# A mixture-of-experts stage with 32 slots per token tile: one gather for six pairs, one scatter product for both halves

## The chip, the cores and the metric

The kernel runs on one core of a Trainium2 chip. The metric is the time of one execution on the device, in microseconds (us); below, times of instructions are in us or ns as each row says. Engines are named as in the profile: PE is TensorE, DVE is VectorE, ACT is ScalarE, POOL is GpSimd, SP is the engine that issues nearly all DMAs here.

## What is computed

A two-layer decoder trunk over 256 tokens of width 1024, in float32. In each layer a token mixer (three head groups, one input and one output projection) is followed by a layer norm, and then by a mixture of 16 experts, each with a gate, an up and a down matrix, which this change is about:

```python
def moe_ffn(h, router_w, router_bias, w_gate, w_up, w_down):
    t = h.reshape(B * L, D)                      # 256 x 1024
    scores = jax.nn.sigmoid(t @ router_w)
    ...                                          # best group of 4 experts, then top 2 in it
    combine = ...                                # 256 x 16, two weights per token
    out = jnp.zeros_like(t)
    for e in range(N_EXPERTS):                   # 16; D_FF = 512
        act = jax.nn.silu(t @ w_gate[e]) * (t @ w_up[e])
        out = out + combine[:, e:e + 1] * (act @ w_down[e])
```

Each of the 16 experts has 6 MB of weights per layer, so some 200 MB of expert weights pass through the core in one execution.

## The kernel before

The tokens stand in two tiles of 128 (`NT = 2`, index `t`). Experts are taken in eight pairs `p` (experts 2p and 2p + 1). A token's place among the tokens of its expert is its slot (`pos`); `CAP` slots per expert are computed (64 for all 256 tokens), so that a pair has 128 slots, and tokens over the cap go through `overflow()` (line 1397), a branch that is taken only if some expert has more than `CAP` tokens.

For a pair, PE's queue has, in this order:

- **gather**: one-hot matrices `G` (token by slot, built on DVE by `slots`) bring the tokens' rows into slot order, transposed, as `xT`. Pairs 0 and 1 have one gather each in plain float32 (`gather`, line 1337). Pairs 2 and 3, 4 and 5, 6 and 7 are gathered two at a time (`gather_two`, line 1316): h is split once into a high and a low half (`halve`), each product is made for both halves, 32 products of 256 columns per gather. ACT and DVE evict the result from PSUM with the norm's gain and offset.
- **gate and up** (tile `gu`): for each of the eight k, two products, one per expert, run side by side in the two column halves of the array, 512 columns each.
- `sT`, two transposes that turn the one-hot matrix to slot by token (`by_slot`); DVE makes it 0/1 and sums the slots' weights into `ws`.
- `aT`, four transposes of silu(gate) * up (`turn`), evicted by ACT as `actT`.
- **down** (tile `y`): 16 products of 512 columns. ACT evicts y * ws rounded (`yt`, high), DVE the rest (`yt`, low) (`split`, line 533).
- **scatter** (tile `sc`, line 1383): for each token tile and each half of the 1024 columns, the transposed one-hot times high and low, two products each (`place`), then DVE adds the result to `z`. The scatter of pair p is put into pair p + 1 (`late`), between its up and its down stage; that of pair 6 stands in the gate stage of pair 7, at `SC_AT`.

Weights come in tiles of 512 KB, 24 per pair: 8 for gate, 8 for up, 8 for down. Most go through a feed of 33 buffers (`fp`, `NFEED`, tile `wf`). `specs` (line 285) fixes their order: all gate tiles of a pair, then up, then down, then the next pair; `more()` issues the next load each time PE is through with a tile, from SP, in that order, and a load waits until its buffer has been read. Some tiles are listed in `EXTRA` instead: `more_extra` loads them during the end of the token mixer into other buffers (tile `wx`), where they wait until they are used. A `wx` tile that PE consumes frees no feed buffer. PE needs two gate tiles for each two steps k (one per expert):

```python
for k in range(KT):
    if k % 2 == 0:
        us = [feed.pop((l, nm, p, k + e)) for e in range(2)]
    for e in range(2):
        mm(b_[64 * e:64 * e + 64], xs[p](k, e), part(us[e], k % 2), ...)
        if k % 2 and type(us[e]) is not list:
            more()
```

PSUM has eight banks, taken in turn by all of these (`bank`). All PE, DVE and ACT instructions are recorded through one helper, so that every row of the profile names its line (L231); the tiles tell them apart. A plain float32 product appears as two MATMUL records, a rounded one or a transpose as one.

Of the kernel before, what the change touches and what calls it, by code (L numbers as in the profile page):

```python
# [17 lines left out]
P = 128  # L18
D = 1024
# [7 lines left out]
CAP = 64  # L27
# [14 lines left out]
EXTRA = ((1, 'd', 1, '22', -4), (1, 'g', 0, '22', -4), (2, 'g', 3, '22', -2), (1, 'g', 2, '4', -1), (1, 'g', 6, '4', -1), (1, 'd', 6, '22', 0), (0, 'u', 3, '22', 2), (0, 'd', 4, '22', 5), (0, 'g', 5, '4', 5), (0, 'u', 0, '22', 6), (2, 'd', 6, '22', 7), (2, 'd', 0, '22', 7), (1, 'd', 4, '22', 7), (2, 'u', 4, '22', 9), (1, 'u', 3, '4', 9), (2, 'd', 1, '4', 9), (2, 'g', 1, '4', 9))  # L42
# [16 lines left out]
TWO = (2, 4, 6)  # L59
AT = {(1, 'g'): 'h', (6, 'u'): 'r'}  # L60
# [175 lines left out]
def trunk_kernel(ctx, tc, x, positions, w_in, gate_up, gate_bias, norm_gain, w_out, ln_mix_g, ln_mix_b,  # L236
# [165 lines left out]
    iota = cp.tile([P, CAP], F32, name="iota")  # L402
    nc.gpsimd.iota(iota, pattern=[[1, CAP]], base=0, channel_multiplier=0, allow_small_or_imprecise_dtypes=True)
    pref = cp.tile([P, E], F32, name="pref")
    nc.gpsimd.iota(pref, pattern=[[-1, E]], base=E, channel_multiplier=0, allow_small_or_imprecise_dtypes=True)
# [7 lines left out]
    rc = cp.tile([P, NT, 16], F32, name="rc")  # L413
    rs = cp.tile([P, NT, 2, 8], F32, name="rs")

    def trig_tables():
# [44 lines left out]
        for i in range(2):  # L461
            dve.tensor_copy(rc[:, :, 8 * i:8 * i + 8], trig4[:, 1])
# [53 lines left out]
    def rope(y, off, nh, t):  # L516
        v = y[:, off:off + nh * 64].rearrange("p (h d) -> p h d", d=64)
        sw = bass.AP(tensor=y.tensor, offset=y.offset + off + 8, ap=[y.ap[0], [64, nh], [-8, 2], [1, 8]])
        ab = t1("rope", (P, 2, 128))
        ra, rb_ = (ab[:, i, 0:nh * 16].rearrange("p (h j) -> p h j", h=nh) for i in range(2))  # L520
        dve.tensor_mul(ra, v[:, :, 0:16], rc[:, t, None, :].to_broadcast([P, nh, 16]))
# [159 lines left out]
    def finish(z, sb, sts, g, b):  # L681

        mv = [sm("mv", 5) for _ in range(NT)]
# [35 lines left out]
    for l in range(DEPTH):  # L719
# [513 lines left out]
        def residual(t, n):  # L1233

            c = slice(512 * n, 512 * n + 512)
            r = whole(t, c)
            dve.scalar_tensor_tensor(r, r, ALPHA, vecs[0][:, c], op0=OP.mult, op1=OP.mult)
            dve.scalar_tensor_tensor(r, vecs[1][:, c], ALPHA, r, op0=OP.mult, op1=OP.add)
            dve.tensor_add(z[t][:, c], z[t][:, c], r)
# [6 lines left out]
        def choose(t):  # L1246
# [24 lines left out]
            else:  # L1271
                mm(pc[:, E:2 * E], strict, hot[:, E:2 * E], start=True, stop=False)
                mm(pc[:, E:2 * E], ones_b, hot[:, 0:E], start=False, stop=True)
# [6 lines left out]
        xs, Gs = {}, {}  # L1280
# [4 lines left out]

        def slots(p, tiles=range(NT), G=None):

            two = p in TWO
            n = 4 if two else 2
            if G is None:  # L1290
                G = t2("G", (P, NT, n, CAP), F32R) if two else t1("G", (P, NT, n, CAP))
            for t in tiles:
                ps_ = pos[:, t * E + 2 * p:t * E + 2 * p + n][:, :, None].to_broadcast([P, n, CAP])
                dve.tensor_tensor(G[:, t], iota[:, None, :].to_broadcast([P, n, CAP]), ps_, op=OP.is_equal)
            for q in range(n // 2):
                Gs[p + q] = (G.bitcast(F32) if two else G)[:, :, 2 * q:2 * q + 2]
            return G

        his, los = [], []

        def halve(t, n):

            c = slice(512 * n, 512 * n + 512)
            if n == 0:
                his.append(t4("hi", (P, D), F32R))
                los.append(t4("lo", (P, D), F32R))
            split(h[t][:, c], his[t][:, c], los[t][:, c])
            if n == 1:
                h[t] = None

        def whole(t, c):
            r = t2("whole")
            dve.tensor_add(r, his[t].bitcast(F32)[:, c], los[t].bitcast(F32)[:, c])
            return r

        def gather_two(p, G):

            xT = [t4("xT", (P, 4, 2 * P)) for _ in range(2)]
            for kk in range(4):
                b_ = bank("xT")  # L1320
                b3 = b_.rearrange("p (a n) -> p a n", a=2)
                for k in (2 * kk, 2 * kk + 1):
                    for i, part in enumerate((his, los)):
                        for t in range(NT):
                            mm(b3[:, k % 2], block(part[t], k), G[:, t].rearrange("p a b -> p (a b)"),
                               start=i + t == 0, stop=i + t == 2)
                for k in (2 * kk, 2 * kk + 1):
                    g_, c_ = affine(k)
                    if kk % 2 == 0:
                        act.activation(xT[k // 4][:, k % 4], b3[:, k % 2], AF.Identity, scale=g_, bias=c_)  # L1330
                    else:
                        dve.tensor_scalar(xT[k // 4][:, k % 4], b3[:, k % 2], g_, c_, op0=OP.mult, op1=OP.add)
                od.free(b_)
            for q in range(2):
                xs[p + q] = lambda k, e, o=q * P: xT[k // 4][:, k % 4, o + 64 * e:o + 64 * e + 64]

        def gather(p, G, between=None):

            xT = t4("xT", (P, KT, P))
            bs = [bank("xT") for _ in range(2)]  # L1340
            parts = [(kk, range(NT)) for kk in range(2)] if p else [(kk, (t,)) for t in range(NT) for kk in range(2)]
            for i, (kk, tiles) in enumerate(parts):
                b3 = bs[kk].rearrange("p (a n) -> p a n", a=4)
                for k in range(4):
                    for t in tiles:
                        mm(b3[:, k], block(h[t], 4 * kk + k),
                           G[:, t].rearrange("p a b -> p (a b)"), start=t == 0 and (p > 0 or k == 0), stop=t == NT - 1)
                if NT - 1 in tiles:
                    for k in range(4):
                        g_, c_ = affine(4 * kk + k)  # L1350
                        if kk == 0:
                            act.activation(xT[:, 4 * kk + k], b3[:, k], AF.Identity, scale=g_, bias=c_)
                        else:
                            dve.tensor_scalar(xT[:, 4 * kk + k], b3[:, k], g_, c_, op0=OP.mult, op1=OP.add)
                    od.free(bs[kk])
                if between and i == 0:
                    between()
            xs[p] = lambda k, e: xT[:, k, 64 * e:64 * e + 64]

        def weights(p):  # L1360
            Gw = t1("Gw", (P, NT, 2, CAP))
            for t in range(NT):
                cs_ = comb[:, t * E + 2 * p:t * E + 2 * p + 2][:, :, None].to_broadcast([P, 2, CAP])
                dve.tensor_mul(Gw[:, t], Gs[p][:, t], cs_)
            return Gw

        def by_slot(Gw):

            b_ = bank("sT")
            for t in range(NT):  # L1370
                tr(b_[:, t * P:(t + 1) * P], Gw[:, t].rearrange("p a b -> p (a b)"))
            sT = t1("sT", (P, L), F32R)
            ws = sm("ws", 1)
            dve.tensor_scalar(sT, b_[:, 0:L], 0.0, None, op0=OP.is_gt)
            dve.tensor_reduce(ws, b_[:, 0:L], AX.X, OP.add)
            od.free(b_)
            return sT, ws

# [4 lines left out]
        def scatter(p, yt, sT, tiles=range(NT)):  # L1383
            if p == 0:
                z.extend(t4("z", (P, D)) for _ in range(NT))
            for t in tiles:
                for n in range(2):
                    b_ = bank("sc")
                    place(b_, t, n, yt, sT)
                    zs = z[t][:, 512 * n:512 * n + 512]  # L1390
                    if p == 0:
                        act.activation(zs, b_, AF.Copy)
                    else:
                        dve.tensor_add(zs, zs, b_)
                    od.free(b_)

        def overflow():
            banks = [bank("ov") for _ in range(6)]
            turns = itertools.cycle(banks)
            with tc.If(rmax > CAP):  # L1400
                hTo = [t2("hTo", (P, 2, L)) for _ in range(4)]
                for t in range(NT):
                    for kk in range(2):
                        ht = whole(t, slice(512 * kk, 512 * kk + 512)).rearrange("p (q i j) -> p q j i", j=2, i=P)
# [8 lines left out]
                for e in range(E):  # L1413
# [22 lines left out]
                    for n in range(2):  # L1436
# [6 lines left out]
                        for t in range(NT):  # L1443
                            zs = z[t][:, 512 * n:512 * n + 512]
# [14 lines left out]
        G = slots(0, (0,))  # L1459

        def second():
            for _ in steps[1]:
                pass
            slots(0, (1,), G)

        gather(0, G, second)
        mm(pc[:, 2 * E:3 * E], ones_b, hot[:, 0:E], start=True, stop=False)
        mm(pc[:, 2 * E:3 * E], ones_b, hot[:, E:2 * E], start=False, stop=True)
# [8 lines left out]
        dve.tensor_reduce(cnt, pc[:, 2 * E:3 * E], AX.X, OP.max)  # L1477
# [3 lines left out]
        late = None  # L1481
# [6 lines left out]
        def begin(t, n):  # L1488
            sb[t, n] = bank("sc")
            mm(sb[t, n], ident, z[t][:, 512 * n:512 * n + 512], start=True, stop=False)  # L1490

        for p in range(E // 2):
            gu = []
            if p == E // 2 - 1:
                Gw = weights(p)
            for nm in ("g", "u"):
                b_ = bank("gu")
# [151 lines left out]
```

## Time and profile before

| | us |
|---|---|
| median of 3 runs (746.40 to 746.79) | 746.45 |
| the profiled execution | 745.53 |
| its span, first to last instruction | 743.8 |
| PE busy in the span | 715.8 |
| DVE busy | 373.4 |
| ACT busy | 255.0 |

Busy time is counted per engine over the span. A matmul's record covers its way through the array, so that records of products that follow each other overlap; where the cost of one more product is wanted, it is the distance between starts that counts. The DMA share of a stretch is the mean busy share of the core's 16 DMA engines.

### The profile page before, as it was taken

The page shows a single profiled execution, that of the slowest core. Times are in us where ns is not written, and L with a number is a line of the kernel's source. Part 1 is how long each engine was busy: PE and PEld are TensorE (multiplying, and loading weights), DVE is VectorE, ACT ScalarE, POOL GpSimd, SP SyncE. Part 2 cuts the span into 40 slices and gives each one's busy share as a digit, 9 for nine tenths or more (in the row PEclk, how much of TensorE's full clock was granted, in tenths as well). Part 3 has the DMA queues.
Part 4 walks back from the last instruction along what each step waited for, and adds up shares of the span by engine and source line. Part 5 has one row for each costly group of instructions (what it writes and reads, how often), then busy time and mean ns, then how long its engine had stood idle before and what let it go on. Part 6 is the DMA issues. An engine that isn't in the chain of part 4 may idle for free. (4 is left out here: it accounts for less than half of the span.)

```text
span 743.8 us, 11218 instructions
## 1 busy us (share of the span) xinstructions
PE 715.8 (96%) x3941; PEld 419.2 (56%) x3941; DVE 373.4 (50%) x986; ACT 255.0 (34%) x527; POOL 43.4 (6%) x67
## 2 busy tenths in 40 slices
PE   7999999999999999999899999999999999999993
PEld 6897977754533533433388888777435344353331
DVE  5887866632312322561488688666231223336405
ACT  5667655422211201210186665563222111111101
POOL 2000001100000002200130000001000000020002
PEclk9999999999999999999999999999999999999997
DMA  8899836889999999999999654569898999999941
GB/s 299 281 392 408 322 135 214 325 312 371 364 343 410 408 410 408 408 409 400 332 387 351 221 176 143 195 207 360 316 380 334 367 408 409 409 408 408 406 177 56
DMA packets 81519, 243.04 MB, mean 327 GB/s; under 512 B 9956, under 2 KB 14120, under 8 KB 81448
## 3 DMA queue, kind: packets, MB, share of 16 engines
q1 hardware_dynamic: 80776, 241.86, 86.2%
q8 instruction: 36, 0.59, 0.3%
q10 hardware_dynamic: 416, 0.26, 0.1%
q14 instruction: 35, 0.29, 0.1%
q0 software_dynamic: 256, 0.03, 0.0%
HBM read 241.08 MB, written 1.05 MB: 326 GB/s over the span
## 5 line engine op out<-in xcount | busy, mean ns | idle before, releaser
L231 PE MATMUL gu<-wf,xT 128*64 128x512 f32 x944 | 224.3, 593 | 3.0 <-PEq L1400 3.0
L231 PEld LDWEIGHTS gu<-wf,xT 128*64 128x64 f32 x944 | 72.8, 137 | 136.8 <-issue 126.9
L231 DVE TENSOR_TENSOR wlo<-wf,whi 128x512 fp32r<-128x512 f32 (+2 forms) x174 | 97.3, 598 | 39.6 <-ACT whi L231 36.9
L231 PE MATMUL y<-wf,actT 128*64 128x512 f32 x456 | 110.7, 596 | 1.4 <-ACT actT L231 1.4
L231 ACT ACTIVATE whi<-wf 128x512 fp32r<-128x512 f32 (+2 forms) x176 | 86.8, 552 | 14.5 <-PE po L231 9.5
L231 DVE TENSOR_TENSOR act<-act,gu 128x512 f32<-128x512 f32 x16 | 11.0, 687 | 141.9 <-PE gu L231 86.5
L231 PE MATMUL pj<-whi,hhi 128*128 128x512 f32 (+2 forms) x224 | 81.7, 365 | 0.0
L231 PE MATMUL pj<-wlo,hhi 128*128 128x512 f32 (+2 forms) x224 | 78.2, 349 | 1.6 <-DVE wlo L231 1.5
L231 PE MATMUL pj<-whi,hlo 128*128 128x512 f32 (+2 forms) x224 | 77.7, 347 | 0.0
L231 DVE SCALAR_TENSOR_TENSOR yt<-y,ws,yt 128x512 fp32r<-128x512 f32 x32 | 23.8, 750 | 106.6 <-ACT yt L231 105.4
L231 PEld LDWEIGHTS y<-wf,actT 128*64 128x64 f32 x456 | 33.8, 137 | 58.5 <-issue 51.8
L231 ACT ACTIVATE yt<-y,ws 128x512 fp32r<-128x512 f32 x32 | 21.8, 688 | 100.6 <-PE y L231 100.1
L231 PEld LDWEIGHTS pj<-whi,hhi 128*128 128x128 f32 x224 | 42.1, 188 | 8.3 <-issue 2.9
L231 PEld LDWEIGHTS pj<-wlo,hhi 128*128 128x128 f32 x224 | 42.2, 188 | 7.1 <-DVE wlo L231 3.4
L231 PEld LDWEIGHTS pj<-whi,hlo 128*128 128x128 f32 x224 | 42.1, 188 | 5.2
L231 ACT ACTIVATE xT<-xT,cols 128x256 f32<-128x256 f32 (+1 forms) x40 | 18.2, 518 | 72.0 <-PE xT L231 72.0
L231 PE MATMUL sc<-yt,sT 128*128 128x512 f32 x128 | 36.7, 414 | 1.8 <-ACT yt L231 1.7
L231 ACT ACTIVATE act<-gu 128x512 f32<-128x512 f32 x16 | 9.6, 597 | 79.5 <-PE gu L231 67.0
L231 PE MATMUL gu<-wx,xT 128*64 128x512 f32 x80 | 36.6, 592 | 0.0
L231 ACT ACTIVATE actT<-aT 128x512 f32<-128x512 f32 x16 | 9.6, 598 | 70.0 <-PE aT L231 70.0
L231 DVE TENSOR_TENSOR z<-z,sc 128x512 f32<-128x512 f32 x48 | 29.7, 679 | 7.7 <-PE sc L231 7.7
L231 PEld LDWEIGHTS sc<-yt,sT 128*128 128x128 f32 x128 | 21.9, 189 | 12.5 <-issue 4.9
(269 smaller groups left out, 966.1 us busy)
## 6 DMA issues: line engine op xcount, KB each, us to landing
wf<-in_w_expert_up_dram SPq DMA_DIRECT2D x120, 512.0 KB, 9.6
wf<-in_w_expert_gate_dram SPq DMA_DIRECT2D x116, 512.0 KB, 7.6
wf<-in_w_expert_down_dram SPq DMA_DIRECT2D x114, 512.0 KB, 10.1
wf<-in_w_in_dram SPq DMA_DIRECT2D x32, 512.0 KB, 9.8
wf<-in_w_out_dram SPq DMA_DIRECT2D x16, 512.0 KB, 10.3
wx<-in_w_expert_down_dram SPq DMA_DIRECT2D x24, 256.0 KB, 6.0
wf<-in_w_in_dram SPq DMA_DIRECT2D x16, 292.0 KB, 5.9
wf<-in_w_in_dram SPq DMA_DIRECT2D x16, 264.0 KB, 4.9
```

Source lines behind the costliest of these rows:

```text
L231: return fn(*a, **kw)
```

## The change

Each expert has 32 slots for each token tile (`CAP = 32`, a pair still has 4 x 32 = 128 slots). So a gather's product for token tile t fills only the slots of t, and nothing is added up over tiles.

- Pairs 0 and 1 share one gather (`gather_first`), pairs 2 to 7 share one (`gather_rest`): 12 experts x 32 slots = 384 columns, for each of 8 k, 2 token tiles and 2 halves. Its first half (n = 0) stands between up and down of pair 1, its second behind the down stage of pair 1. ACT evicts the columns of pairs 2 to 5, DVE those of 6 and 7.
- A slot now belongs to one token tile, so the low half of a slot's row can be kept in the row of the other tile's slot: `by_tile` makes two tiles `yt`, and one product per token tile and column half brings back the sum of high and low. For that ACT evicts y twice, and DVE does four operations on 32 partitions in the place of one on 128. The last pair keeps `split` and two products.
- The first two steps of a gate stage can be put ahead: `gate(p + 1, FILL[0])` and `gate(p + 1, FILL[1])` put step k = 0 and k = 1 of the next pair ahead of this pair's down stage (pair 0 does three).
- In pair 1 no scatter is made; pair 2 makes those of pairs 0 and 1.
- `EXTRA` has 16 tiles instead of 17: 12 of pair 1 (7 before), none of pair 2 (6 before), 4 of pair 0 as before. `specs` stays.
- h is no longer thrown away after the split, so `residual` reads it in place of adding the halves (one DVE operation less, four times a layer); z stands in four tiles.

```diff
-CAP = 64
+CAP = 32
-EXTRA = (..., (2, 'g', 3, '22', -2), ..., (2, 'd', 6, '22', 7), (2, 'd', 0, '22', 7), ..., (2, 'u', 4, '22', 9), ..., (2, 'd', 1, '4', 9), (2, 'g', 1, '4', 9))
+EXTRA = (..., (1, 'u', 1, '22', -2), ..., (1, 'u', 6, '22', 7), (1, 'u', 7, '22', 7), ..., (1, 'u', 5, '22', 9), ..., (1, 'u', 2, '4', 9))
+FILL = (1, 2)
+FILL_0 = (2, 3)
...
+        def gather_rest(n, Gs):
+            xq.extend(t4("xq", (P, 2, 4 * P)) for _ in range(2))
+            xd.append(t4("xd", (P, 4, 2 * P)))
             for kk in range(4):
+                k = 4 * n + kk
+                for t in range(NT):
+                    b_ = bank("xT")
+                    for i, part_ in enumerate(parts[t, n]):
+                        mm(b_[:, 0:12 * CAP], block(part_, kk), Gs[t].rearrange("p e i -> p (e i)"), start=i == 0, stop=i == 1)
+                    evict(act, xq[k // 2][:, k % 2], t, b_[:, 0:8 * CAP], k)
+                    evict(dve, xd[n][:, kk], t, b_[:, 8 * CAP:12 * CAP], k)
+                    od.free(b_)
...
+        def by_tile(ps, ys, ws):
+            for y in ys:
+                act.activation(y, ps, AF.Copy, scale=ws)
+            for q in range(P // CAP):
+                t = q % NT
+                r = slice(q * CAP, (q + 1) * CAP)
+                o = slice((q + 1 - 2 * t) * CAP, (q + 2 - 2 * t) * CAP)
+                dve.scalar_tensor_tensor(ys[t][o], ps[r], ws[r], ys[t].bitcast(F32)[r], op0=OP.mult, op1=OP.subtract)
...
                 for n in range(2):
                     b_ = bank("sc")
-                    place(b_, t, n, yt, sT)
+                    mm(b_, sT[:, t * P:(t + 1) * P], yt[n][t])
...
+        def gate(p, upto):
+            if p not in gates:
+                gates[p], done_k[p] = bank("gu"), 0
+            while done_k[p] < upto:
+                step(p, "g", gates[p], done_k[p])
+                done_k[p] += 1
...
-                (gather_two if p + 1 in TWO else gather)(p + 1, G)
+                if len(late) > 1:
+                    scatter(*late.pop(0))
+                scatter(*late[0], (0,))
+                gate(p + 1, FILL[0])
                 turn()
-                scatter(*late)
+                scatter(*late.pop(), (1,))
+                gate(p + 1, FILL[1])
...
                 if k == 3:
                     yt[n] = [t2("yt", dt=F32R) for _ in range(2)]
-                    split(py[n], *yt[n], scale=ws)
+                    if final:
+                        split(py[n], *yt[n], scale=ws)
+                    else:
+                        by_tile(py[n], yt[n], ws)
...
+            if p == 1:
+                gather_rest(1, Gs)
+            late.append((p, yt, sT))
```

How it moves instructions, at two places. First PE in pair 6 and the start of pair 7 of layer 0 (`gu` gate and up, 16 steps of two products a pair; `sc` scatter of the pair before; `y` down). Before:

```order
L231 MATMUL gu<-wf,xT 64x512 x32
L231 MATMUL sT<-ident,Gw 128x128 x2
L231 MATMUL sc<-yt,sT 128x512 x4
L231 MATMUL aT<-ident,act 128x128 x4
L231 MATMUL sc<-yt,sT 128x512 x4
L231 MATMUL y<-wf,actT 64x512 x16
L231 MATMUL gu<-wf,xT 64x512 x12
L231 MATMUL sc<-yt,sT 128x512 x8
```

and with the change:

```order
L234 MATMUL gu<-wf,xd 64x512 x28
L234 MATMUL sT<-ident,Gw 128x128 x2
L234 MATMUL sc<-yt,sT 128x512 x2
L234 MATMUL gu<-wf,xd 64x512 x2
L234 MATMUL aT<-ident,act 128x128 x4
L234 MATMUL sc<-yt,sT 128x512 x2
L234 MATMUL gu<-wf,xd 64x512 x2
L234 MATMUL y<-wf,actT 64x512 x16
L234 MATMUL gu<-wf,xd 64x512 x8
L234 MATMUL sc<-yt,sT 128x512 x4
```

The two `gu` rows of two products ahead of `y` are steps 0 and 1 of pair 7's gate; before, all of pair 7's gate came behind pair 6's `y`. The scatters have half the products.

Second, PE at the end of pair 1 and the start of pair 2 with the change (`xT<-G,hl` is half of `gather_rest`, `xq` its result for pairs 2 to 5):

```order
L234 MATMUL y<-wf,actT 64x512
L234 MATMUL xT<-G,hl 128x384 x16
L234 MATMUL gu<-wf,xq 64x512 x32
L234 MATMUL sT<-ident,Gw 128x128 x2
L234 MATMUL sc<-yt,sT 128x512 x6
L234 MATMUL gu<-wf,xq 64x512 x2
L234 MATMUL aT<-ident,act 128x128 x4
L234 MATMUL sc<-yt,sT 128x512 x2
L234 MATMUL gu<-wf,xq 64x512 x2
L234 MATMUL y<-wf,actT 64x512 x16
```

Before, the scatter of pair 0 and a `gather_two` stood between up and down of pair 1, and nothing between pair 1's down stage and pair 2's gate.

## Rows read from the trace of the kernel before

**Rows 1.** The page, parts 1 and 2: busy time of the engines; DMA busy tenths by slice.
```profile
PE 715.8 (96%) x3941; PEld 419.2 (56%) x3941; DVE 373.4 (50%) x986; ACT 255.0 (34%) x527; POOL 43.4 (6%) x67
...
DMA  8899836889999999999999654569898999999941
```

**Rows 2.** Busy time by stretch, layer 0: us, engines (count), clock, DMA share, GB/s.
```profile
208.00:222.00 14.00, 14.00 (x66) 4.42 (x62) 1.81 (x4) 2.84 (x5) 0.00 (x0) 1.00 0.97 352
222.00:333.00 111.00, 111.00 (x554) 47.41 (x554) 43.04 (x79) 15.56 (x26) 9.10 (x13) 1.00 1.03 409
```

**Rows 3.** Timeline, SP, layer 0: start of loads, us, what, count (pair 7's gate, up).
```profile
310.90 9.30 SPq L331 DMA_DIRECT2D wf<-in_w_expert_gate_dram  x8
321.15 9.60 SPq L331 DMA_DIRECT2D wf<-in_w_expert_up_dram  x8
```

**Rows 4.** Timeline, PE, layer 0, pairs 6 and 7: start us, us, what, count.
```profile
309.54 13.90 PE L231 MATMUL gu<-wf,xT 128*64 128x512 f32 x64
...
323.57 1.18 PE L231 MATMUL sc<-yt,sT 128*128 128x512 f32 x4
...
326.04 7.09 PE L231 MATMUL y<-wf,actT 128*64 128x512 f32 x32
332.96 5.32 PE L231 MATMUL gu<-wf,xT 128*64 128x512 f32 x24
338.21 2.11 PE L231 MATMUL sc<-yt,sT 128*128 128x512 f32 x8
341.80 5.37 PE L231 MATMUL gu<-wf,xT 128*64 128x512 f32 x24 [1.48 <-PEq L1400]
...
366.17 1.52 PE L231 MATMUL sc<-yt,sT 128*128 128x512 f32 x4 [0.87 <-ACT yt L231]
```

**Rows 5.** DMA issues: count, KB each, median us from issue to landing.
```profile
wf<-in_w_expert_gate_dram SPq DMA_DIRECT2D x116, 512.0 KB, 7.6
...
wx<-in_w_expert_gate_dram SPq DMA_DIRECT2D x8, 256.0 KB, 3.0
```

**Rows 6.** Timeline, PE, layer 0: half of the gather of pair 1.
```profile
172.06 2.05 PE L231 MATMUL xT<-G,h 128*128 128x128 f32 x16
```

**Rows 7.** Timeline, PE, layer 0: gather of pairs 2 and 3, a scatter, pair 2's start.
```profile
194.98 0.49 PE L231 MATMUL xT<-G,hi 128*128 128x256 f32 x2
...
198.91 0.60 PE L231 MATMUL aT<-ident,act 128*128 128x128 f32 x4
199.27 2.09 PE L231 MATMUL sc<-yt,sT 128*128 128x512 f32 x8
...
208.21 0.59 PE L231 MATMUL gu<-wf,xT 128*64 128x512 f32 x1
```

**Rows 8.** Timeline, PE, layer 0: start of pair 0.
```profile
155.58 1.94 PE L231 MATMUL gu<-wf,xT 128*64 128x512 f32 x8
```

**Rows 9.** ACT by form: count, busy us, mean ns, idle before it.
```profile
L231 ACT ACTIVATE xT<-xT,cols 128x256 f32<-128x256 f32 x24 | 12.2, 560 | 51.4 <-PE xT L231 51.4
...
L231 ACT ACTIVATE actT<-aT 128x512 f32<-128x512 f32 x16 | 9.6, 598 | 70.0 <-PE aT L231 70.0
...
L231 ACT ACTIVATE kiT<-tr 128x256 f32<-128x256 f32 x2 | 0.8, 383 | 6.2 <-PE tr L231 6.2
...
L231 ACT ACTIVATE rT<-tr 16x256 f32<-16x256 f32 x2 | 0.7, 356 | 0.0
```

**Rows 10.** DVE by form, the same columns.
```profile
L231 DVE SCALAR_TENSOR_TENSOR yt<-y,ws,yt 128x512 fp32r<-128x512 f32 x32 | 23.8, 750 | 106.6 <-ACT yt L231 105.4
```

**Rows 11.** Timeline, PE, the last matmuls.
```profile
731.25 1.52 PE L231 MATMUL sc<-yt,sT 128*128 128x512 f32 x4 [0.85 <-ACT yt L231]
```

**Rows 12.** Busy time by stretch, the end, columns as in rows 2.
```profile
736.00:744.00 8.00, 0.00 (x0) 0.00 (x0) 4.53 (x5) 0.35 (x1) 2.61 (x2) 0.51 0.35 131
```

**Rows 13.** Timeline, PE, the first projections.
```profile
5.88 3.79 PE L231 MATMUL pj<-wf,hT 128*128 128x292 f32 x8
...
9.95 1.15 PE L231 MATMUL pj<-wf,hT 128*128 128x292 f32 x4
```

More of the change, by code (lines that the diff above doesn't have):

```diff
@@ L679, in split_t, with finish @@
                 od.free(b_)
-    def finish(z, sb, sts, g, b):
+    def finish(sb, sts, g, b):
+        z = [t4("z", (P, D)) for _ in range(NT)]
         mv = [sm("mv", 5) for _ in range(NT)]
@@ L1278, in trunk_kernel @@
         comb3 = comb.rearrange("p (t e) -> p t e", t=NT)
-        xs, Gs = {}, {}
+        xs = {}
         def affine(k):
             return (lnM[:, l, g, k:k + 1] for g in range(2))
[L1286 to L1297, printed above, removed]
@@ L1337, in gather @@
[L1337 to L1358, printed above, removed]
@@ new lines, in gather_first @@
+        def gather_first(between):
+            xT = [t4("xT", (P, 4, 2 * P)) for _ in range(2)]
+            G = t1("G", (P, NT, 4, CAP))
+            bs = [bank("xT") for _ in range(4)]
+            for t in range(NT):
+                if t:
+                    between()
+                slots(G[:, t], t, 0)
+                for j in range(4):
+                    b4 = bs[j].rearrange("p (a t n) -> p a t n", a=2, t=NT)
+                    for i in range(2):
+                        mm(b4[:, i, t], block(h[t], 2 * j + i), G[:, t].rearrange("p a b -> p (a b)"))
+                    if t == NT - 1:
+                        for i in range(2):
+                            k = 2 * j + i
+                            g_, c_ = affine(k)
+                            d = xT[k // 4][:, k % 4].rearrange("p (e t i) -> p t e i", t=NT, i=CAP)
+                            src = b4[:, i].rearrange("p t (e i) -> p t e i", i=CAP)
+                            if i == 0:
+                                act.activation(d, src, AF.Identity, scale=g_, bias=c_)
+                            else:
+                                dve.tensor_scalar(d, src, g_, c_, op0=OP.mult, op1=OP.add)
+                        od.free(bs[j])
+            for q in range(2):
+                xs[q] = lambda k, e, o=q * P: xT[k // 4][:, k % 4, o + 64 * e:o + 64 * e + 64]
@@ L1383, in scatter @@
         def scatter(p, yt, sT, tiles=range(NT)):
-            if p == 0:
-                z.extend(t4("z", (P, D)) for _ in range(NT))
+            if p == 0 and not z:
+                z.extend([t2("z") for _ in range(2)] for _ in range(NT))
             for t in tiles:
@@ L1463, in second @@
                 pass
[L1464 to L1468, printed above, removed]
+        gather_first(second)
+        mm(pc[:, 2 * E:4 * E], ones_b, hot)
         dve.tensor_mul(comb, hot, sc)
@@ L1480, in trunk_kernel @@
         dve.tensor_copy(cnti, cnt)
-        late = None
+        late = []
         rmax = None
@@ L1489, in begin, with step @@
             sb[t, n] = bank("sc")
-            mm(sb[t, n], ident, z[t][:, 512 * n:512 * n + 512], start=True, stop=False)
+            mm(sb[t, n], ident, z[t][n], start=True, stop=False)
+        FIN = E // 2 - 1
+        gates, done_k, us, Gs = {}, {}, {}, []
+        def step(p, nm, b_, k):
+            if k % 2 == 0:
+                us[nm] = [feed.pop((l, nm, p, k + e)) for e in range(2)]
+            for e in range(2):
+                mm(b_[64 * e:64 * e + 64], xs[p](k, e), part(us[nm][e], k % 2), start=k == 0, stop=k == KT - 1)
+                if k % 2 and type(us[nm][e]) is not list:
+                    more()
+            if (p, nm) == (FIN, "u") and k in BEGIN:
+                begin(*((0, 0), (1, 0), (0, 1))[BEGIN.index(k)])
+            if (p, nm, k) == (FIN, "g", SC_AT):
+                scatter(*late.pop())
+            if (p, nm, k) == (FIN, "g", OVER_AT):
+                overflow()
+            if (p, nm) == (1, "u") and k in HALVE_U:
+                halve(HALVE_U.index(k), 0)
+            if (p, nm) == (FIN - 1, "u") and k % 2:
+                residual(k // 4, k // 2 % 2)
@@ L1521, in trunk_kernel @@
-            dve.tensor_mul(av, av, gu[1])
-            od.free(*gu)
-            sT, ws = by_slot(Gw)
+            gate(p, KT)
+            av = t2("act")
+            act.activation(av, gates[p], AF.Silu)
+            if not final:
+                Gw = weights(p)
+            if p == 1:
+                for t in range(NT):
+                    Gs.append(t2("G", (P, 12, CAP), F32R))
+                    slots(Gs[t], t, 4)
+            bu = bank("gu")
+            for k in range(KT):
+                step(p, "u", bu, k)
@@ L1525, in turn @@
+            dve.tensor_mul(av, av, bu)
+            od.free(gates[p], bu)
+            sT, ws = by_slot(Gw, final)
             def turn():
@@ L1535, in trunk_kernel @@
             made = []
-            if p == E // 2 - 1:
+            if final:
                 begin(1, 1)
                 turn()
-            elif p + 1 in xs:
-                scatter(*late, (0,))
+            elif p == 0:
+                gate(1, FILL_0[0])
                 turn()
-                scatter(*late, (1,))
-            elif not late:
-                gather(p + 1, G, turn)
-            else:
-                (gather_two if p + 1 in TWO else gather)(p + 1, G)
+                gate(1, FILL_0[1])
+            elif p < LATER:
+                gather_rest(0, Gs)
+                turn()
+            else:
+                if len(late) > 1:
+                    scatter(*late.pop(0))
+                scatter(*late[0], (0,))
+                gate(p + 1, FILL[0])
                 turn()
-                scatter(*late)
+                scatter(*late.pop(), (1,))
+                gate(p + 1, FILL[1])
             aT, = made
@@ L1551, in trunk_kernel @@
             yt = [None, None]
-            us = [feed.pop((l, "d", p, i)) for i in range(8)]
-            final = p == E // 2 - 1
+            ud = [feed.pop((l, "d", p, i)) for i in range(8)]
             for i in range(8):
```

168 lines of the change are left out of this document (74 added, 94 removed).

## The prediction, made before the changed kernel was run

> **What bounds the kernel now.** The page's busy times come first: PE is busy for 715.8 of 743.8 us and the next engine, DVE, for 373.4 [rows 1]. That says that a product less is time less, as long as nothing else becomes late. Whether something does is read from the DMA slices: 9 in the long stretches where experts run, 5 or 6 only in the middle mixer. So the second view is the busy time by stretch [rows 2]. From pair 2's start to pair 7 PE is busy for 111.00 of 111 us, and at the same time the DMA share is 1.03 at 409 GB/s. Two resources are full at once, and the reader should ask how much lead the second has.
>
> A load is 512 KB (524,288 bytes); at 409 GB/s it takes 1.28 us, and SP's rows say the same: the eight up loads of pair 7 are issued 10.25 us behind the eight gate loads [rows 3]. A pair has 24 loads, 30.7 us. PE needs 332.96 - 309.54 = 23.4 us for a pair without a gather [rows 4]. So the feed loses 7.3 us on PE in each pair, and lives on what the 33 buffers held before. What is left of it in pair 7: its gate loads begin to be issued at 310.90, the second 1.3 later lands about 7.6 us after its issue [rows 5], near 320, and is used at 332.96. The lead at the end is some 13 us, and **the change takes about 17 us of products out of each layer.** The question is whether they become time or waiting.
>
> **Products removed, per layer.** Pair 1's own gather: its 8 products (16 records) are half of it and take 2.05 us [rows 6], so 4.1. A two-pair gather: 198.91 - 194.98 = 3.93 us for 32 products [rows 7], 0.123 each; three are 11.8. In their place 32 products of 384 columns in the place of 256: 32 x 0.123 x 1.5 = 5.9. Net 5.9 saved. Scatter: 8 products take 2.11 us [rows 4], 0.26 each; seven scatters lose 4 each: 28 x 0.26 = 7.3. Together 17.3 us per layer, 34.6 in both. The first gather has 16 products as before.
>
> **Term A, pairs 0 and 1.** Before they take 208.21 - 155.58 = 52.6 us [rows 7, 8]. PE's work changes by -4.1 (gather of pair 1), -2.1 (the scatter of pair 0 moves to pair 2), -3.9 (gather of 2 and 3) and +5.9: -4.2. Two waits come in. First, `actT` stands on ACT behind eight evictions of 128x256; such a one is busy for 12.2 / 24 = 0.51 us, `actT` for 0.60 [rows 9]. They end some 8 x 0.51 + 0.6 + 0.6 (until the first group is done) = 5.3 us after the gather's start, while PE has 2.95 of gather and 0.36 of transposes: pair 1's `y` waits 2.0. Second, the other half of the gather needs eight banks in turn behind `y`, whose two banks are held until `by_tile` is through: eight DVE operations of 512 columns on 32 partitions. The trace has them on 128 partitions, 23.8 / 32 = 0.744 us [rows 10]. What 32 partitions cost is not shown; the ends are a quarter, 0.19, and all of it, 0.744. The nearest row is ACT's 16x256 eviction at 356 ns beside 383 for 128x256 [rows 9]: columns count, partitions hardly. I take 0.744. Eight are 6.0; with 0.4 until they start and 0.6 for the two last groups pair 2 starts 7.0 after `y`, of which 2.95 is work: a wait of 4.1. A is -4.2 + 2.0 + 4.1 = +1.9.
>
> **Term B, the feed from pair 2's start.** Buffers are full then (pairs 0 and 1 free 32 in some 54 us, and 32 x 1.28 = 41). They hold pair 2's 24 tiles and 9 of pair 3. Pair 7's first step needs the 121st and 122nd tile, so 89 have to be loaded; before, six of pair 2 lay in other buffers, and it was 83. The first buffer is free after four products, 1.7 us [rows 4]; a load without a queue takes up to 3.0 [rows 5]. So pair 7's first gate tiles are there 89 x 1.28 + 1.7 + 3.0 = 118.6 us after pair 2's start. The same count for before gives 110.9, and the rows 320 - 208.2 = 112: it is not too slow. The order of the loads is unchanged, so pair 6's eight down tiles have to land ahead of these two.
>
> **Term C, PE on the way there.** With the change step 0 of pair 7's gate stands in PE's queue ahead of pair 6's `aT`, the second half of a scatter and `y`. PE gets to such a place 13.9 (gate and up) + 1.5 (six products of scatters) = 15.4 us after pair 2's start, then every 23.4 - 4 x 0.26 = 22.4: 105.0 for pair 7. It **waits 118.6 - 105.0 = 13.6 us per layer**, by the same count some 5 of it at pair 6's first step (65 tiles: 87.9 against 82.6), the other 8.3 at pair 7's. All work behind it waits too, pair 6's down stage included, though its tiles have landed. So this place is 7.1 us of `y` earlier than where the data would be needed.
>
> **Term D, from that landing to the layer's end.** Two steps 1.7, aT 0.36, two scatter products 0.52: 2.6 to `y`. From there it was 366.17 + 1.52 - 326.04 = 41.65 [rows 4]; two steps (1.7) and four scatter products (1.04) are gone from it, and the scatter of pair 6 in pair 7's gate comes 3.7 us after `y`, while `by_tile` is done 6.4 after it: +2.7. Sum 44.2. Pair 2's start to the end is then 118.6 + 44.2 = 162.8, before 367.69 - 208.21 = 159.5: +3.3. With A: **+5.2 per layer**.
>
> **The clock.** After a stretch without products PE may come back slower. The last product ends at 732.77 [rows 11], and the granted clock of 736 to 744 is 0.51 [rows 12]: the lower level (1.2 GHz) within some microseconds of rest. At the program's start the same eight records take 0.47 us each, and 0.29 later [rows 13]. A wait of 8.3 us in pair 7 should bring that: eight such records more at the lower level cost 8 x 0.18 = 1.4. Ends: nothing, if the clock holds, and twice as much, if it falls at pair 6's wait as well. I take 1.5. Sum 6.7 per layer, 13.4 for two.
>
> **Edits at nothing:** `residual` without the halves' sum, the small DVE operations for `ws` and `Gw`, ACT's second eviction of `y`: DVE is busy for 47 and ACT for 43 of 111 us in this stretch [rows 2], and the readers come later, apart from the places in A and D. If that cover went, it would be a few operations of 0.2 to 0.7 us per pair. With the reference's inputs no expert gets more than 22 tokens of one tile, so the overflow branch isn't taken.
>
> **A rule beside the rate.** The rate is 409 GB/s over 111 us of a full queue [rows 2], and falls to 352 in the stretch before it, where three of the tiles used free no feed buffer. The Trainium skill ("DMA: Bandwidth & Descriptors", section "Where 436 GB/s comes from") gives two limits: about 358 GB/s for a core's reads from memory and 435 for the ports. By 435 (an estimate from that page) the 89 tiles would be there 6.7 us earlier per layer and the sum would be about 746; by 358, 16 later and 790. The trace agrees with neither: it lies between.
>
> **The rivals.**
> 1. *Faster: the feed isn't late.* If pair 7's tiles are there by 105.0 (a tile in 1.13 us, 464 GB/s, or as good, if more tiles were ahead at pair 2's start than I count), PE never waits, and the sum is -17.3 + 6.1 + 2.7 = -8.5 per layer: 729. For it: my count stands on the buffers' number and one rate. Against it: 1.03 of DMA share at 409. It decides from a lead of 13.6 us. 0.12.
> 2. *The clock never falls:* +5.2 per layer, 757. For it: the waits are short, and no row shows how long a rest takes to lower it. 0.24.
> 3. *DVE's operations on 32 partitions cost a quarter:* both waits for `by_tile` (4.1 and 2.7) go, 6.7 - 6.8 per layer: about 746, no difference. Against it rows 9. 0.09.
> 4. *Landings are later still,* 3 us per layer, since in pair 7 other loads (norm constants, next layer's first weights) share the queue: 766. 0.07.
> 5. *The feed runs at 352 GB/s,* as in the stretch 208 to 222 [rows 2]: 1.49 us a tile, 18.6 per layer more, 797. Against it the 111 us behind. 0.02.
>
> **How the numbers follow.** The sum stands on the profiled execution of 745.53, 0.9 below the median of the runs: 745.53 + 13.4 + 0.9 = 760. My forecast has 0.46. The range takes in cases 2 and 4, half of 3 and the upper end of the clock: 746 to 769; outside lie 1, 5 and the rest of 3. A measurement here tells 0.2%, 1.5 us, from no change. Faster: case 1 and a little of 3, 0.14. Same: most of 3, 0.06. Slower: 0.80.
>
> **What would show it.** In the changed kernel's profile PE idles ahead of `gu<-wf,xd`, ended by a DMA, 5 and 8 us in each layer, with the DMA share near 1 from pair 2 on; `yt` operations of 32x512 at 0.75 us; `xT<-G,hl` of the second half waiting for DVE for some 4 us; a clock below 1.00 just behind pair 7's wait. It is wrong if pair 7's gate starts without a wait for its tiles, or if pair 2's start to the layer's end takes under 158 us.

## The result, and the profile after

The changed kernel takes 784.25 us (median of 4 runs, 782.98 to 785.55) against 746.44 before: a ratio of 1.0506, interval 1.0485 to 1.0526, 37.8 us slower. The profiled execution took 782.98 us, its span is 781.2. The direction was forecast, the size was not: 760 was expected, 769 was the range's upper end.

The page of the changed kernel, parts 1 and 2 (answers to [rows 1]):

```profile
PE 709.4 (91%) x3689; PEld 391.3 (50%) x3689; DVE 438.9 (56%) x1115; ACT 270.6 (35%) x555; POOL 44.0 (6%) x72
...
PEclk9999999999999998988999999999998999998887
DMA  8999656979499999999997644577975999999911
```

PE is busy for 6.4 us less than before and the span is 37.4 longer: the removed products became waits. PE's busy time fell by no more than that, with 34.6 us of products gone, in part because records are longer at a lower clock (its mean over the span is 0.961, before 0.995). The DMA slices show the feed full in the later part of both expert stretches, as before. Which waits it is stands in the list of waits of PE, first of the changed kernel, then of the one before (us in total, times, longest):

```profile
PE gu L234 <- DMA wf<-in_w_expert_gate_dram: 18.2, 4, 5.5
PE gu L234 <- PEq L1420: 11.7, 2, 5.9
PE xT L234 <- DVE yt L234: 7.7, 4, 2.5
PE sc L234 <- DVE yt L234: 4.3, 2, 2.2
PE y L234 <- ACT actT L234: 4.3, 4, 1.5
```

```profile
PE gu L231 <- PEq L1400: 3.0, 2, 1.5
...
PE y L231 <- ACT actT L231: 1.4, 2, 0.7
```

Five waits are new or larger: for gate tiles (the forecast's term C), **for PE's own sequencer (PEq in the profile) at the overflow branch (11.7 in the place of 3.0, in no term)**, for `yt` in two places (A and D), and for `actT` (A).

Where they stand in layer 0, the PE timeline of the changed kernel, from the end of pair 1 to pair 2 and from pair 6 to the layer's end:

```profile
197.78 0.64 PE L234 MATMUL y<-wf,actT 128*64 128x512 f32 x1 [1.46 <-ACT actT L234]
...
204.80 2.35 PE L234 MATMUL xT<-G,hl 128*128 128x384 f32 x12
208.53 0.59 PE L234 MATMUL xT<-G,hl 128*128 128x384 f32 x2 [1.39 <-DVE yt L234]
211.60 0.98 PE L234 MATMUL xT<-G,hl 128*128 128x384 f32 x2 [2.47 <-DVE yt L234]
212.51 15.01 PE L234 MATMUL gu<-wf,xq 128*64 128x512 f32 x64
...
301.48 3.25 PE L234 MATMUL gu<-wf,xd 128*64 128x512 f32 x4 [3.85 <-DMA wf<-in_w_expert_gate_dram]
...
332.52 3.25 PE L234 MATMUL gu<-wf,xd 128*64 128x512 f32 x4 [5.05 <-DMA wf<-in_w_expert_gate_dram]
335.70 1.12 PE L234 MATMUL aT<-ident,act 128*128 128x128 f32 x4
336.47 1.20 PE L234 MATMUL sc<-yt,sT 128*128 128x512 f32 x2
337.60 1.08 PE L234 MATMUL gu<-wf,xd 128*64 128x512 f32 x4
338.51 7.04 PE L234 MATMUL y<-wf,actT 128*64 128x512 f32 x32
345.38 3.60 PE L234 MATMUL gu<-wf,xd 128*64 128x512 f32 x16
348.91 0.50 PE L234 MATMUL sc<-yt,sT 128*128 128x512 f32 x1
351.58 1.26 PE L234 MATMUL sc<-yt,sT 128*128 128x512 f32 x3 [2.17 <-DVE yt L234]
358.75 6.69 PE L234 MATMUL gu<-wf,xd 128*64 128x512 f32 x24 [5.91 <-PEq L1420]
...
384.39 1.52 PE L234 MATMUL sc<-yt,sT 128*128 128x512 f32 x4 [0.81 <-ACT yt L234]
```

| stretch, layer 0 | before | forecast | after |
|---|---|---|---|
| pair 0's start to pair 2's start | 52.6 | 54.5 | 55.6 |
| pair 2's start to pair 7's first gate product | 124.7 | 118.6 | 120.0 |
| from there to the layer's last product | 34.7 | 44.2 | 53.4 |
| pair 2's start to the end | 159.5 | 162.8 | 173.4 |

(Before, pair 7's gate comes behind pair 6's `y`, with the change its step 0 ahead of it.) In layer 1 pair 2 starts at 595.39 and the last product ends at 770.19, 174.8 us behind it, where it was 159.5. Two more pieces lie ahead of pair 0: 1.3 us in layer 0 and 0.9 in layer 1, of which 0.8 each in the first gather, whose second tile waits 0.7 for its one-hot on DVE.

Up to pair 7's first gate product the layer came out as worked out, to 1.1 and 1.4 us. **The rest of the miss, 9.2 us, lies behind that product.** The rows above say where: 6.0 from that product to `y` (332.52 to 338.51) where 2.6 was forecast, 2.2 at the scatter (forecast 2.7), then 5.9 "<-PEq", and the 24 records behind it in 6.69 in the place of 5.37 [rows 4].

The branch itself, by PE's sequencer, in both kernels (duration ns min/median/max, first and last start):

```profile
L1400 PEldq COMPARE_BRANCH  x2: 6075/6094/6112, 335.6 to 700.6; - x2
```

```profile
L1420 PEldq COMPARE_BRANCH  x2: 6072/6131/6190, 352.4 to 735.5; - x2
```

It takes 6.1 us in both. Before, the sequencer started on it at 335.6, when the array still had products until 340.3; only 1.48 showed [rows 4]. Now it starts at 352.4, just when the last scatter products are let go, and nothing is queued: 5.9 show.

One record of the traces bears on what happens in these 6 us. The line of an instruction queue in the DMA view of the changed kernel, 352 to 359 us (packets, MB, share of the 16 engines' time):

```profile
q8 instruction: 1, 0.02, 1.0%
```

This packet has 16 KB and starts 3.6 us behind the branch's start. The same stands in both layers of both kernels, and 3.5 to 3.8 us behind the start in all 20 branches of the ten traced kernels that have the branch. The Trainium skill ("Runtime: NRT & Kernel Launch", section "Instruction fetch mechanics") says that a taken branch whose target lies outside the prefetched window has to fetch it by DMA before anything goes on. The branch skips the overflow code, and these packets fit that. That the packet is PE's, and that its fetch is the whole of the 6.1 us, is not shown.

The granted clock, busy time by stretch (columns as in [rows 2]):

```profile
212.50:215.00 2.50, 2.50 (x9) 0.86 (x10) 2.50 (x10) 0.56 (x1) 0.00 (x0) 0.56 0.00 0
222.00:333.00 111.00, 102.11 (x459) 35.45 (x456) 54.57 (x103) 16.52 (x28) 8.63 (x13) 0.96 1.03 409
332.50:339.00 6.50, 6.48 (x18) 2.37 (x20) 2.30 (x4) 0.60 (x1) 0.00 (x0) 0.61 1.03 411
352.80:365.40 12.60, 6.69 (x26) 2.20 (x25) 2.93 (x6) 0.60 (x1) 0.00 (x0) 0.73 1.03 400
```

0.56 at the start of pair 2, 0.61 behind the wait for pair 7's tiles and 0.73 behind the branch: PE has been at rest for 1.39 and 2.47 us before the first, with two gather products between, and for 5.05 and 5.91 us before the others. Each mean lies between the two levels, 1.2 and 2.4 GHz, so PE came back at the lower one and rose again. The feed runs at 409 GB/s as before, but moves nothing in the first of these stretches: at pair 2's start its buffers are full.

### The profile page after: what moved, and what is told of

The parts are those of the page before. It is cut to its first block, busy times and chain, and to the rows that moved or that the text cites. A ratio compares the mean times of both kernels' runs of the same rounds, so it can differ in the third digit from the quotient of the medians.

```text
span 781.2 us, 10844 instructions
## 1 busy us (share of the span) xinstructions
PE 709.4 (91%) x3689; PEld 391.3 (50%) x3689; DVE 438.9 (56%) x1115; ACT 270.6 (35%) x555; POOL 44.0 (6%) x72
## 5 line engine op out<-in xcount | busy, mean ns | idle before, releaser
L234 DVE SCALAR_TENSOR_TENSOR yt<-y,ws,yt 32x512 fp32r<-32x512 f32 (+1 forms) x116 | 86.7, 748 | 115.5 <-ACT yt L234 114.0
L234 PE MATMUL y<-wf,actT 128*64 128x512 f32 x480 | 113.7, 594 | 4.3 <-ACT actT L234 4.3
L234 PE MATMUL gu<-wf,xq 128*64 128x512 f32 x512 | 117.5, 610 | 0.0
L234 PE MATMUL gu<-wf,xd 128*64 128x512 f32 x256 | 71.7, 663 | 29.9 <-DMA wf<-in_w_expert_gate_dram 18.2
L234 ACT ACTIVATE yt<-y,ws 128x512 fp32r<-128x512 f32 x60 | 36.6, 688 | 110.0 <-PE y L234 110.0
L234 PEld LDWEIGHTS gu<-wf,xq 128*64 128x64 f32 x512 | 36.1, 140 | 73.2 <-issue 69.0
L234 PEld LDWEIGHTS y<-wf,actT 128*64 128x64 f32 x480 | 35.8, 137 | 68.4 <-issue 55.8
L234 PEld LDWEIGHTS gu<-wf,xd 128*64 128x64 f32 x256 | 19.9, 150 | 72.7 <-issue 40.0
L234 PE MATMUL gu<-wf,xT 128*64 128x512 f32 x160 | 50.0, 595 | 0.0
```

Of the source, the lines that this page charges most:

```text
L234: return fn(*a, **kw)
```

## The experiments

Each is a change of one of the two kernels; times are medians, all against the kernel before on the same chip.

**1. No steps ahead of the down stage.**

```diff
-FILL = (1, 2)
+FILL = (0, 0)
```

> Steps 0 and 1 of the next pair's gate no longer stand ahead of a pair's down stage (pairs 2 to 6). Theory: the place of these steps costs pair 6's down stage, 6.9 us, in each layer, since it then runs inside the wait for pair 7's tiles; with it by_tile of pair 6 is done before the scatter needs it. Pair 7's first gate product starts about 120 us after pair 2's start as now, but with y already done: 11 to 14 us less per layer, 756 to 762. Rival: the later gate tiles, which land 1.28 us apart, are the bound, and the wait only moves behind y: under 3 us less per layer, 778 to 784.

Measured: 759.28 (ratio 1.0179, 1.0151 to 1.0206), 25.0 less than the change, 12.5 per layer. PE in pairs 6 and 7:

```profile
325.56 7.89 PE L234 MATMUL y<-wf,actT 128*64 128x512 f32 x32 [0.23 <-ACT actT L234]
332.92 3.54 PE L234 MATMUL gu<-wf,xd 128*64 128x512 f32 x10
336.64 2.35 PE L234 MATMUL gu<-wf,xd 128*64 128x512 f32 x8 [0.19 <-DMA wf<-in_w_expert_gate_dram]
339.20 1.93 PE L234 MATMUL gu<-wf,xd 128*64 128x512 f32 x6 [0.20 <-DMA wf<-in_w_expert_gate_dram]
341.06 1.20 PE L234 MATMUL sc<-yt,sT 128*128 128x512 f32 x4
346.60 3.68 PE L234 MATMUL gu<-wf,xd 128*64 128x512 f32 x8 [4.34 <-PEq L1420]
```

Pair 7's first gate product starts at 332.92, as late as before the edit (332.52), but pair 6's `y` is through. The place of the step was the cost, not the tiles' lateness as such; with it go the scatter's wait for `yt` (2.2) and 1.6 of the branch. Behind it PE takes gate tiles as they land (waits of 0.2 each), and the branch still shows 4.3.

**2. Pair 6 without `by_tile`.** `by_slot` and `scatter` take pair 6 as they take the last pair: `split`, high and low, two products.

```diff
-                    if final:
+                    if p in (6, 7):
                         split(py[n], *yt[n], scale=ws)
...
+                    if p in (6, 7):
+                        place(b_, t, n, yt, sT)
+                    else:
+                        mm(b_, sT[:, t * P:(t + 1) * P], yt[n][t])
```

> Pair 6 uses split and two products per scatter as before the change, in the place of by_tile's eight DVE operations. Theory: these eight operations hold the scatter in pair 7's gate 2.2 us, PE's sequencer can't run ahead, and so the branch behind it, 6.1 us on the sequencer in both kernels, is exposed by 5.9 in the place of 1.5; the clock is lower behind it. Expected 6 to 8 us less per layer, 768 to 772, the branch's wait back near 1.5. Rival: the branch takes long to show because the DMA queues are full at its new place, and the sequencer is held by late tiles anyway: only the 2.2 goes and four products (1.0) come, 1 us less per layer, 782.

Measured: 771.19 (1.0331, 1.0312 to 1.0350), 13.1 less, 6.5 per layer. PE in pair 7:

```profile
349.08 2.11 PE L234 MATMUL sc<-yt,sT 128*128 128x512 f32 x8
353.64 7.07 PE L234 MATMUL gu<-wf,xd 128*64 128x512 f32 x24 [2.46 <-PEq L1423]
```

The wait ahead of the scatter is gone, and the branch's exposed part falls from 5.9 to 2.5 (near 1.5 was expected). The queues to memory are as full as in the change (the feed isn't touched), so the rival falls: DVE's eight operations held PE's sequencer, and that exposed the branch.

**3. The change without the branch,** and **4. the kernel before without it.** The call of `overflow()` is taken out.

> The overflow branch is left out (with these inputs it is never taken). Theory: the wait of 5.9 us behind the scatter goes whole, with 1.3 to 2.7 of slower products behind it: 7 to 8.6 less per layer, 767 to 770. Rival: pair 7's up tiles land too late to use this, and the wait comes back as one for DMA: under 3 per layer, 778 to 783.

> The kernel before without the overflow branch. Theory: there the sequencer came to the branch 4.6 us ahead of the array, and only 1.5 us showed: 3 us less for both layers, 743.5. Rival: more of it is hidden cost (later waits take it up, or the clock): no change, 746, or over 6 less, 740.

Measured: 767.87 (1.0289, 1.0272 to 1.0307), 16.4 less than the change, 8.2 per layer; and 743.12 (0.9959, 0.9947 to 0.9972), 3.1 less than the kernel before. In the kernel before the exposed wait is worth what the rows say, 1.5 per layer. In the change the rows give 11.7 for the two waits and 2.3 for faster products behind them, 14.0 for both layers; the spans of the profiled executions differ by 13.9. The medians differ by 2.4 more, which no row shows. The 24 records behind the branch's place in run 3, layers 0 and 1 (6.69 and 8.06 in the change):

```profile
352.74 5.37 PE L234 MATMUL gu<-wf,xd 128*64 128x512 f32 x24
...
728.72 7.07 PE L234 MATMUL gu<-wf,xd 128*64 128x512 f32 x24
```

**5. `split` in pairs 1 and 6.** As experiment 2 with `(1, 6, 7)`.

> Pairs 1 and 6 use split and two products per scatter, the fill stays. Against pair 6 alone (771.2): theory: the second half of the gather no longer waits 1.4 and 2.5 us for by_tile's eight DVE operations, pair 2 starts 3.5 us earlier, and since the feed is counted from pair 2's start (buffers full by then), all that follows is 3.5 earlier: 764 for both layers. Rival: the feed's end is fixed by something earlier than pair 2's start, and the 3.5 come back as a longer wait at the first gate steps of pairs 6 and 7: 771, no change.

Measured: 760.67 (1.0191, 1.0174 to 1.0209), 10.5 less than with pair 6 alone, 5.3 per layer. Pair 2 starts at 207.91 instead of 212.51, 4.6 earlier, and pair 7's first gate product at 326.85: 118.9 behind it. The gain arrives at the end: the feed is counted from pair 2's start, and the rival falls. The 4.6 are 0.7 more than the two waits for `yt`: the half gather, which no wait breaks now, takes 2.97 us in the place of 3.85, from a start 0.1 later. Behind it the clock no longer falls: pair 2's 64 gate and up records take 13.95 (15.01 in the change, 16.55 with pair 6 alone), and pair 7's first product comes 1.7 us earlier behind pair 2's start than with pair 6 alone (120.6).

```profile
207.91 13.95 PE L234 MATMUL gu<-wf,xq 128*64 128x512 f32 x64
...
326.85 3.25 PE L234 MATMUL gu<-wf,xd 128*64 128x512 f32 x4 [6.73 <-DMA wf<-in_w_expert_gate_dram]
```

**6. Both: no steps ahead, `split` in pairs 1 and 6.**

> Both edits: no steps ahead of the down stage, split in pairs 1 and 6. Against no fill alone (759.3): theory: pair 2 starts 3.5 us earlier per layer, and as PE and feed are nearly level there, this is kept: 752; pair 6's split gives nothing more, since the scatter did not wait there any more. Rival: PE is the bound from pair 2 to pair 6 without the fill, and four products more in each of two scatters cost 2 us per layer: 756.

Measured: 743.61 (0.9968, 0.9957 to 0.9978): 2.6 faster than the kernel before. 752 was expected. Of the 4.2 us per layer beyond that 1.3 are pair 2's start (4.8 earlier than in experiment 1). In layer 0, 1.7 more come between there and pair 7's first gate product (118.9 us, in experiment 1 120.6: the clock at pair 2 again), and 1.1 behind that product; in layer 1 it is 1.1 and 4.0. I held that `split` in pair 6 gives nothing once the scatter shows no wait. PE in this run, then DVE and the branch in experiment 1, then the branch here:

```profile
204.59 3.04 PE L234 MATMUL xT<-G,hl 128*128 128x384 f32 x16
207.56 13.95 PE L234 MATMUL gu<-wf,xq 128*64 128x512 f32 x64
...
333.87 1.93 PE L234 MATMUL gu<-wf,xd 128*64 128x512 f32 x6 [0.21 <-DMA wf<-in_w_expert_gate_dram]
335.73 2.11 PE L234 MATMUL sc<-yt,sT 128*128 128x512 f32 x8
340.26 5.31 PE L234 MATMUL gu<-wf,xd 128*64 128x512 f32 x15 [2.43 <-PEq L1423]
```

```profile
333.98 6.12 DVE L234 SCALAR_TENSOR_TENSOR yt<-y,ws,yt 32x512 fp32r<-32x512 f32 x8 [6.38 <-ACT yt L234]
```

```profile
L1420 PEldq COMPARE_BRANCH  x2: 5974/6072/6170, 340.3 to 712.4; - x2
```

```profile
L1423 PEldq COMPARE_BRANCH  x2: 6031/6099/6167, 333.9 to 698.1; - x2
```

In experiment 1 the last gate tiles ahead of the scatter are taken at 339.20, `by_tile` ends at 340.1, and PE's sequencer gets to the branch at 340.3, while the array still works through products in its queue and the scatter until 342.3: a lead of 2.0. Here the last such tiles are taken at 333.87, the sequencer gets there at 333.9, and the array is done at 337.8: 3.9. So the late tiles hold the sequencer in both, and `by_tile` had held it for some 1.0 us more (0.4 in layer 1) without a wait of the array to show for it; the other 0.9 of lead is the longer scatter. The branch's part falls from 4.34 to 2.43, and the 24 records behind it from 8.26 us to 7.07: 3.1 in layer 0, less the 0.9 that the scatter takes more (2.11, before 1.20).

**7 and 8. Thirty feed buffers in the place of 33,** in the changed kernel and in the one before.

> The changed kernel with 30 feed buffers instead of 33. Theory: pair 7's first gate tiles land when 92 instead of 89 loads are done, 3 x 1.28 = 3.8 us later in each layer: 784.3 + 7.7 = 792. Rival: the waits at the fills come from the transfers' own latency or from the order of loads, not from the count of buffers: 784, no change.

> The kernel before with 30 feed buffers. Theory: its lead at pair 7 is some 13 us, three buffers take 3.8 of it: no change, 746. Rival: the lead is smaller than the rows say, or thin places elsewhere (the mixer's weights) show: 748 to 754.

Measured: 791.37 (1.0611, 1.0593 to 1.0629), 7.1 more than the change; and 746.37 (0.9999, 0.9989 to 1.0008), nothing. The count of buffers sets when pair 7 can start in the changed kernel, three transfers of 1.28 us per layer, and the kernel before had lead for them.

**9. The transposes in the middle of the gather,** on top of experiment 6.

```diff
+                if kk == 1 and between:
+                    between()
...
-                gather_rest(0, Gs)
-                turn()
+                gather_rest(0, Gs, turn)
```

> On top of no fill and split in pairs 1 and 6 (743.6): in pair 1 the four transposes stand in the middle of the first half of the gather, so that actT is fifth and not ninth among ACT's evictions. Theory: pair 1's y no longer waits 1.47 us for actT, pair 2 starts that much earlier, and since feed and PE are level behind it, this is kept: 740.7. Rival: the array then waits for the transposes' input (DVE's product of act and gu) in the middle of the gather instead, or the gain is lost at the feed: 743.6.

Measured: 739.24 (0.9906, 0.9891 to 0.9921), **7.1 us faster than the kernel before, and the fastest with the whole computation.** PE in pair 1; `y` has no wait behind these rows:

```profile
193.03 1.65 PE L234 MATMUL xT<-G,hl 128*128 128x384 f32 x8
194.52 0.60 PE L234 MATMUL aT<-ident,act 128*128 128x128 f32 x4
194.87 1.65 PE L234 MATMUL xT<-G,hl 128*128 128x384 f32 x8
```

**10. The same without the branch.**

> The same, and the overflow branch is left out (never taken with these inputs). Theory: 2.4 us of wait and 1.7 of slower products behind it go in each layer, less what the late tiles of pair 7's up stage take back: 3 to 4 per layer, 733 to 735. Rival: pair 7's tiles are the bound by then and the wait only changes its name: 740.

Measured: 738.19 (0.9888, 0.9873 to 0.9904), 1.0 less for both layers, where 3 to 4 per layer were expected, and the two intervals overlap: the rival is nearer. Pair 7's down stage now waits for its tiles:

```profile
351.54 3.81 PE L234 MATMUL y<-wf,actT 128*64 128x512 f32 x14 [0.69 <-ACT actT L234]
355.58 2.79 PE L234 MATMUL y<-wf,actT 128*64 128x512 f32 x10 [0.23 <-DMA wf<-in_w_expert_down_dram]
```

Of 3.8 us that the branch and the products behind it took in layer 0 of experiment 9, `y` and its scatters give back 1.5 here (6.8 us from 351.54 to 358.30, there 5.3). In this version most of the branch lies beside the feed.

**11. Steps put ahead only for pairs 3 to 5,** on top of experiment 6.

> No fill for pairs 6 and 7, steps 0 and 1 of pairs 3 to 5 put ahead as in the change; split in pairs 1 and 6. Theory: a step that is put ahead costs only where its tiles are late; for pairs 3 to 5 they have landed, so the time is that without any fill, or up to 1 us less per layer, since the waits of 0.2 to 0.3 for actT are covered: 742 to 744. Rival: putting steps ahead costs by itself (order of releases and loads): 746 or more.

Measured: 743.10 (0.9955, 0.9942 to 0.9969), as experiment 6 within what can be told. A step put ahead costs nothing where its tiles have landed.

## Why the prediction was wrong

Point by point, in the order of its steps:

- **Products removed: right.** In the changed kernel the scatters and gathers have the forecast number and length (two scatter products 0.70, half of a gather 3.03).
- **Term A: right in its mechanisms.** Waits of 1.46 for `actT` (forecast 2.0) and 1.39 + 2.47 for `yt` (4.1). The stretch is 3.0 longer than before, forecast 1.9: the gather's second half takes 3.85 without its waits, not 2.95, since each wait breaks the run of its products, and small gaps make the rest. A DVE operation on 32 partitions costs as one on 128, which decides rival 3:

```profile
L234 DVE SCALAR_TENSOR_TENSOR yt<-y,ws,yt 32x512 fp32r<-32x512 f32 x112 | 83.7, 748 | 103.9 <-ACT yt L234 102.4
```

- **Term B: the count was right, but went to the wrong instant and left out the clock.** Pair 7's step 0 starts 120.0 after pair 2's start in layer 0 and 120.9 in layer 1, forecast 118.6, at 409 GB/s. Without the waits for `yt` in pair 1 (experiment 5) it is 118.9 and 119.1. The difference is TensorE's clock: it fell in those waits, pair 2 began at a granted 0.56, freed its first buffers later, and until then the feed stood. And 118.6 was to be the landing of both tiles of that step, while 332.52 is the start of its first product: the second waits for a transfer more, so that the four records take 3.25 us where the next step's four take 1.08. Experiments 7 and 8 bear the count out, and rivals 1 and 5 fall. (One slip without effect: by the prediction's own 16 us per layer, the sum at 358 GB/s is 792, not 790.)
- **Term C: right in its mechanism.** Waits for gate tiles of 3.85 and 5.05 in layer 0, with the second tile of each step inside the row that follows; the forecast was 5 and 8. Experiment 1 gives the price of the place, 12.5 per layer with what hangs on it.
- **Term D failed.** It took the stretch of the kernel before and added 2.7 for the scatter's wait, as if a wait of PE in the queue cost its own length. The scatter's wait was 2.2, but it also took away the lead with which the sequencer hid the overflow branch. That branch stood in [rows 4] as a wait of 1.48 "<-PEq", and I read it as a small fixed cost instead of the rest of a longer one. Its cost rose by 4.4 per layer. Experiments 2, 3 and 4 show it.
- **The clock was undersized:** 1.5 per layer was taken, and 2.9 the upper end, for the waits at the tiles alone. At pair 7's it cost about 1.8 (335.70 to 338.51 holds what takes 1.96 in pair 3, and some 0.9 of the 3.25 are neither the step nor the transfer). At pair 6's it fell too (0.54 over 300.0 to 307.5), off the path, since pair 7's tiles were waited for behind it. Two falls were not foreseen: at pair 2's start, most of the 1.4 (layer 0) and 2.3 (layer 1) in B, and behind the branch, 1.3 in layer 0 and 2.7 in layer 1 (8.06 for the 24 records).
- **What had no term:** 1.3 and 0.9 us ahead of pair 0.

In layers 0 and 1: 5.2 and 5.2 forecast without the clock; 1.1 and 1.1 more in A; 1.4 and 2.3 in B; 9.2 and 9.7 from pair 7's first product to the layer's last; 1.3 and 0.9 ahead of pair 0: 18.2 and 19.2, together the 37.4 by which the span is longer. The 9.2 are 3.4 up to `y` (1.3 the second tile's transfer, the rest mostly clock), 4.4 the branch, 1.3 the clock behind it and 0.6 in the four scatter products and rows beside them, less 0.5 of the scatter's wait. Rival 2 fell: the clock went lower at four places in each layer, not never. Rival 4, later landings, is worth 1.4 to 2.3 and not 3, and not for its reason: without the clock's fall at pair 2 it is 0.3 to 0.5.

## What to carry to other kernels

A wait that the profile puts down to an engine's sequencer (a branch, here) can be what is left of a longer one: look up the whole duration and ask what queued work hides the rest, before adding any wait ahead of it. A short wait can cost again behind it, through the clock: here two waits of 1.39 and 2.47 us in a gather made the whole feed some 1 to 2 us later. Work that is put ahead of other work in an in-order queue is only free where its data have landed; when two resources are both full, count the feed up to the place that the moved instruction has now. The same saving of products was worth having: with no steps put ahead, without the slow eviction in the two pairs where PE waits for it, and with the transposes earlier, it gives 739.2 against 746.4.

## What the runs showed that was not expected

- PE's compare-and-branch lasts 6.0 to 6.2 us in each kernel shown here that has it; how much shows goes by how far the sequencer is ahead: in layer 0 1.5 in the kernel before, 2.4 in experiments 6 and 9, 4.3 in 1, 5.9 in the change.
- Costs on one path do not add up. Without the branch the changed kernel gains 16.4 us, and the best version 1.0, since there pair 7's tiles land no earlier than needed.
- What stops the sequencer need not show as a wait of the array: in experiment 1 no row has PE waiting for `by_tile`, and yet it held the sequencer for some 1.0 us in layer 0.
- The granted clock was 0.61 in the 6.5 us behind a rest of 5.05, and 0.56 in 2.5 us behind rests of 1.39 and 2.47. The same 24 records behind the branch took from 5.37 us (the kernel before, and layer 0 without the branch) to 8.3 us (experiment 1).
